# Reading and writing the 288 columns of every weight product from the last to the first

## The chip, the cores and the metric

The kernel runs on one core of one Trainium2 chip. The metric is the device time of one launch in microseconds (us). Before the change it is 2207.99 us, the median of three runs (2207.06 to 2208.8).

## The reference

The program computes one layer of a decoder trunk for two groups of tokens: a prompt of 256 tokens and a sample group of 8 x 4 = 32 tokens. With the width 2048 the layer is

```python
x = x + 0.5 * rmsnorm(swiglu(rmsnorm(x, g[0]), ffn1_w_in, ffn1_w_out), g[1])
m, sg, sh = hybrid_mixer(rmsnorm(x, g[2]), ...)     # gated linear attention (4 heads) and HGRN2 (8 heads)
x = x + rmsnorm(m, g[3])
x = x + 0.5 * rmsnorm(swiglu(rmsnorm(x, g[4]), ffn2_w_in, ffn2_w_out), g[5])
```

`swiglu(x, w_in, w_out)` is `(silu(gate) * up) @ w_out` with `gate, up = split(x @ w_in)` and an inner width of 5632. The mixer projects with `mix_w_in` (2048 to some 7200 columns), evaluates two recurrences over the tokens, normalises, gates, and projects back with `mix_w_out`. Outputs are the new activations of both groups and the final states of both recurrences. Everything is fp32, and the result has to be accurate to fp32 inputs.

## The kernel before

**Layout.** All 288 tokens (256 of the prompt, then 32 of the sample group) are handled together. Activations lie with the model dimension on the 128 partitions and the tokens along the row: `x[k]` is a 128 x 288 tile, k from 0 to 15. A weight product takes a 128 x 128 piece of a weight matrix as the stationary operand and a 128 x 288 activation tile as the moving operand, and accumulates 128 x 288 sums in a PSUM tile.

**Three products for one.** TensorE's reduced fp32 format (fp32r in the profile, `F32R` in the code) drops low bits. So each weight piece is split by ScalarE and VectorE into a high part and a low part (lines 100 and 101, tile `wh`), and so is each activation tile (`xh`, `xl` for the layer's input, `hh`, `hl` for the inner activations of the feed-forward part). `mm3` (lines 594 to 598) issues three products for each weight piece and activation tile: high x high (line 596), high weight x low activation (597) and low weight x high activation (598). All go into the same accumulator `dst`; the first of a chain starts the sum anew, the last closes it. The operands `parts[0]` and `parts[1]` are the whole rows of the high and the low tile, `dst` the first 288 columns of an accumulator of 512.

**Blocks.** `block` (from line 583) computes 512 output columns of a matrix: four accumulators of 128 output rows, and for each up to 16 steps over the inner dimension. When the last step of an accumulator is issued, `evac` reads it with VectorE or ScalarE. Blocks are named after what they compute, and these names stand in the profile: `gate`, `up` and `out` for the feed-forward parts, `qk`, `v`, `hfq`, `hi`, again `gate`, and `mo` for the mixer. `Fill.products` uses the same `mm3` for a few products that are issued early, at the border of two parts of the layer (names with `fill`). The scans of the recurrences, the transposes, the norms' sums and the small low-rank projection have product calls of their own, with lines of their own, among them line 437 (column sums for a norm), line 863 (sums at the end, in full fp32) and line 1385 (the sample group's state update, in fp32r).

**Order.** Weights come in units of 512 KB on SP's DMA queue, three raw units ahead (`Weights.fill`), and are split up to four units ahead of their use (`Weights.ahead`). The tile framework issues each engine's instructions by a planner from their dependencies and priorities; `tc.issue_after` puts some instructions behind others on the same engine by hand, and the `tick` callbacks spread the scans' work between the weight products.

Of the kernel before, what the change touches and what calls it, by code (L numbers as in the profile page):

```python
# [130 lines left out]
def trunk_kernel(ctx, tc, x_prompt, x_sample, state_gla, state_hgrn, norm_gains, f1_in, f1_out, f2_in, f2_out,  # L131
# [3 lines left out]
    V, S, G, PE = nc.vector, nc.scalar, nc.gpsimd, nc.tensor  # L135
# [33 lines left out]
    def mmtile(name):  # L169
        return mmp.tile([P, 512], F32, name=name, tag="mm")  # L170
# [416 lines left out]
    def block(name, nk, rhs, evac, width=512, tick=None, tail=1, hold=False, most=99, fill=None, late=0, byk=(), lag=0, skip=()):  # L587

        nf, per = width // P, 1024 // width
        nu = nk // per  # L590
        ps = [mmtile(f"{name}_{f}") for f in range(nf)]
        ws = [W.next() for _ in range(EARLY // per)] if fill else []

        def mm3(dst, w, f, k, parts, start, stop):
            a, c = k % per, slice(f * P, f * P + P)
            yield lambda: PE.matmul(dst, w[0][:, a, c], parts[0], start=start, stop=False)  # L596
            yield lambda: PE.matmul(dst, w[0][:, a, c], parts[1], start=False, stop=False)  # L597
            yield lambda: PE.matmul(dst, w[1][:, a, c], parts[0], start=False, stop=stop)  # L598

        def mm(w, f, k):  # L600
            if not fill or f or k >= EARLY:
                for ready in mm3(ps[f][:, 0:T], w, f, k, rhs(k), k == 0, k == nk - 1):
                    product[0] = ready().ins

        if fill:
            fill.products(lambda dst, k, parts, stop: mm3(dst, ws[k // per], 0, k, parts, k == 0, stop), ps[0][:, 0:T])
        for u in range(nu - tail):
            w = ws.pop(0) if ws else W.next()
            if u not in byk:
                for f in range(nf):  # L610
                    for k in range(u * per, (u + 1) * per):
                        mm(w, f, k)
                    if tick is not None and f % 2:
                        tick(u * per + f // 2)
            for k in range(u * per, (u + 1) * per) if u in byk else ():
                if fill and k < UPDATED:

                    fs = range(1 if k < EARLY else 0, nf)
                    threes = [list(mm3(ps[f][:, 0:T], w, f, k, rhs(k), k == 0, False)) for f in fs]
                    for three in threes:  # L620
                        three[0]()
                        product[0] = three[2]().ins
                    with tc.issue_after(product[0]):
                        for three in threes:
                            product[0] = three[1]().ins
                elif k < late:

                    threes = [list(mm3(ps[f][:, 0:T], w, f, k, rhs(k), k == 0, False)) for f in range(nf)]
                    for ready in [r for t in threes for r in t[:2]] + [t[2] for t in threes]:
                        product[0] = ready().ins  # L630
                else:
                    for f in range(nf):
                        mm(w, f, k)
                if tick is not None:
                    tick(k)
            if u not in skip and not (lag and u == nu - tail - 1):
                W.ahead(most)
            if fill and u == 5:
                fill.scaled()
        ws = [W.next() for _ in range(tail)]  # L640
        ks = range((nu - tail) * per, nk)
        ticked = 0
        for f in range(nf):
            for k in ks:
                mm(ws[k // per - (nu - tail)], f, k)
            ins = evac(f, fill.total(ps[f][:, 0:T]) if fill and f == 0 else ps[f][:, 0:T])
            while tick is not None and (ticked + 1) * nf <= (f + 1) * len(ks):
                tick(ks[ticked])
                ticked += 1
            if lag and f == lag:  # L650
                with tc.issue_after(ins):
                    W.ahead(most)
        if not hold:
            W.ahead()
# [1078 lines left out]
```

## Time and profile before

| | |
|---|---|
| median of three runs | 2207.99 us |
| span of the profiled execution, first to last instruction | 2206.5 us |
| mean granted TensorE clock | 1.000 |
| TensorE busy | 2198.2 us |
| VectorE busy | 1385.7 us |
| ScalarE busy | 1020.1 us |
| read from HBM | 363.75 MB |

The profile gives no other time of the profiled execution than its span; the span is 1.5 us below the median of the runs. In the rows that follow, PE is TensorE, PEld its weight loads, DVE is VectorE, ACT ScalarE and POOL GpSimd; L597 is line 597 of the kernel. A row of instructions by line gives the engine, the operation, the tile that is written and the tiles that are read, the count, and the shortest, median and longest duration. A row of the timeline gives the start, the duration, and what ran. Products overlap in the engine's pipeline and their ends are modelled, so the duration of one is longer than the distance from its start to the start of the next.

### The profile page before, as it was taken

How to read it: one execution, taken by the hardware profiler on the slowest of the kernel's cores; microseconds unless marked ns; L12 is line 12 of the kernel's file. 1: busy time of each engine (PE TensorE's matmuls, PEld its weight loads, DVE VectorE, ACT ScalarE, POOL GpSimd, SP SyncE). 2: the span in 40 equal slices, each digit the busy share in tenths (PEclk: the TensorE clock that was granted, in tenths of full speed). 3: DMA queues.
4: the chain of work that ended last, by engine and by line, in shares of the span. 5: the costliest groups of instructions: out<-in, count | busy, mean ns of one | idle time of the engine just before them, and what ended most of it. 6: DMA issues, size and time to landing. Idle time of an engine off the chain costs nothing.

```text
span 2206.5 us, 43225 instructions
## 1 busy us (share of the span) xinstructions
PE 2198.2 (100%) x17828; PEld 2182.2 (99%) x17828; DVE 1385.7 (63%) x2253; ACT 1020.1 (46%) x1537; POOL 180.0 (8%) x327
## 2 busy tenths in 40 slices
PE   9999999999999999999999999999999999999998
PEld 9999999999999999999999999999999999999998
DVE  7545546555555568888888755844555466556646
ACT  6443433343344345655676654543333333333344
POOL 2000000000000001233210000000000020122005
PEclk9999999999999999999999999999999999999999
DMA  7655555555555554667566564555555565666555
GB/s 223 174 166 171 169 168 170 171 165 171 172 166 180 179 166 142 194 207 216 173 189 176 176 190 135 169 167 171 171 166 170 172 176 172 180 179 179 172 164 161
DMA packets 227334, 384.87 MB, mean 174 GB/s; under 512 B 21362, under 2 KB 60864, under 8 KB 227136
## 3 DMA queue, kind: packets, MB, share of 16 engines
q1 hardware_dynamic: 213872, 365.02, 55.1%
q0 software_dynamic: 10992, 16.77, 2.8%
q8 instruction: 140, 2.29, 0.4%
q10 hardware_dynamic: 2272, 0.31, 0.1%
q14 instruction: 58, 0.48, 0.1%
HBM read 363.75 MB, written 11.80 MB: 170 GB/s over the span
## 4 chain that ended last, share of the span: by engine, by line
PE 98%; DVE 1%; ACT 1%; issue 0%; POOL 0%; DVEq 0%; ACTq 0%; POOLq 0%
PE gate L597 10%; PE gate L596 10%; PE gate L598 10%; PE up L597 8%; PE out L597 8%; PE up L596 8%; PE up L598 8%; PE out L596 8%; PE out L598 8%; PE hfq L596 2%; PE hfq L597 2%; PE mo L597 2%; PE hfq L598 2%; PE mo L596 1%; PE mo L598 1%; PE hi L597 1%
## 5 line engine op out<-in xcount | busy, mean ns | idle before, releaser
L101 DVE TENSOR_TENSOR wh<-raw,wh 128x1024 fp32r<-128x1024 f32 (+1 forms) x676 | 821.7, 1217 | 610.2 <-ACT wh L100 609.1
L100 ACT ACTIVATE wh<-raw 128x1024 fp32r<-128x1024 f32 (+1 forms) x676 | 711.0, 1053 | 943.1 <-PE gate L598 295.2
L597 PE MATMUL gate<-xl,wh 128*128 128x288 f32 x1660 | 490.1, 297 | 0.0
L598 PE MATMUL gate<-xh,wh 128*128 128x288 f32 x1660 | 483.6, 293 | 0.0
L596 PE MATMUL gate<-xh,wh 128*128 128x288 f32 x1660 | 483.0, 292 | 0.0
L597 PE MATMUL out<-hl,wh 128*128 128x288 f32 x1408 | 419.2, 298 | 0.0
L597 PE MATMUL up<-xl,wh 128*128 128x288 f32 x1408 | 419.2, 298 | 0.0
L598 PE MATMUL up<-xh,wh 128*128 128x288 f32 x1408 | 411.6, 292 | 0.0
L598 PE MATMUL out<-hh,wh 128*128 128x288 f32 x1408 | 411.5, 292 | 0.0
L596 PE MATMUL out<-hh,wh 128*128 128x288 f32 x1408 | 409.3, 291 | 0.0
L596 PE MATMUL up<-xh,wh 128*128 128x288 f32 x1408 | 409.3, 291 | 0.0
L596 PEld LDWEIGHTS gate<-xh,wh 128*128 128x128 f32 x1660 | 313.7, 189 | 0.8 <-DVE u L691 0.4
L598 PEld LDWEIGHTS gate<-xh,wh 128*128 128x128 f32 x1660 | 311.4, 188 | 0.2 <-DVE wh L101 0.2
L597 PEld LDWEIGHTS gate<-xl,wh 128*128 128x128 f32 x1660 | 310.2, 188 | 0.5
L596 PEld LDWEIGHTS out<-hh,wh 128*128 128x128 f32 x1408 | 266.8, 189 | 0.2 <-DVE y L782 0.2
L596 PEld LDWEIGHTS up<-xh,wh 128*128 128x128 f32 x1408 | 266.7, 189 | 0.0
L598 PEld LDWEIGHTS up<-xh,wh 128*128 128x128 f32 x1408 | 264.5, 188 | 0.0
L598 PEld LDWEIGHTS out<-hh,wh 128*128 128x128 f32 x1408 | 264.5, 188 | 0.0
L597 PEld LDWEIGHTS up<-xl,wh 128*128 128x128 f32 x1408 | 263.8, 187 | 0.0
L597 PEld LDWEIGHTS out<-hl,wh 128*128 128x128 f32 x1408 | 263.7, 187 | 0.0
L782 DVE TENSOR_TENSOR y<-out,y 128x288 f32<-128x288 f32 x287 | 120.7, 452 | 82.1 <-PE out L598 81.1
L739 POOL DMA_DIRECT2D xT<-b x64 | 37.1, 586 | 757.3 <-PE gate L598 566.7
(417 smaller groups left out, 2559.1 us busy)
## 6 DMA issues: line engine op xcount, KB each, us to landing
raw<-in_ffn_w_in_dram SPq DMA_DIRECT2D x350, 512.0 KB, 3.6
raw<-in_ffn_w_out_dram SPq DMA_DIRECT2D x176, 512.0 KB, 3.6
raw<-in_mix_w_in_dram SPq DMA_DIRECT2D x64, 512.0 KB, 4.3
raw<-in_mix_w_in_dram SPq DMA_DIRECT2D x96, 256.0 KB, 3.2
raw<-in_mix_w_out_dram SPq DMA_DIRECT2D x32, 512.0 KB, 3.7
out_dram<-s POOLq DMA_DIRECT2D x32, 256.0 KB, 2.9
s<-in_state_gla_dram SPq DMA_DIRECT2D x16, 256.0 KB, 5.9
s<-in_state_hgrn_dram SPq DMA_DIRECT2D x16, 256.0 KB, 5.6
```

What stands on the lines that cost most here:

```text
L100: i1 = self.nc.scalar.activation(h[:, a, c], raw[:, a, c], AF.Copy).ins
L101: i2 = self.nc.vector.tensor_tensor(l[:, a, c], raw[:, a, c], h[:, a, c].bitcast(F32), op=ALU.subtract).ins
L596: yield lambda: PE.matmul(dst, w[0][:, a, c], parts[0], start=start, stop=False)
L597: yield lambda: PE.matmul(dst, w[0][:, a, c], parts[1], start=False, stop=False)
L598: yield lambda: PE.matmul(dst, w[1][:, a, c], parts[0], start=False, stop=stop)
L739: queues[n % len(queues)].dma_start(dst[q * TS:(q + 1) * TS, 4 * g:4 * g + 4, :, cols].rearrange("p k t c -> p (k t) c"), b32[rows, q])
L782: V.tensor_tensor(y[k], ps, y[k], op=ALU.add)
```

## The change

In each of the three products of `mm3`, the moving operand and the accumulator are both given with their columns reversed. Column 287 is read first and its sum is written to column 287 first, then 286, down to 0. The same elements are multiplied and added in the same sums; the stationary operand is given as before. `mm3` serves all weight products of the layer, those of `Fill` included. Products with calls of their own are not touched.

```diff
         def mm3(dst, w, f, k, parts, start, stop):
             a, c = k % per, slice(f * P, f * P + P)
-            yield lambda: PE.matmul(dst, w[0][:, a, c], parts[0], start=start, stop=False)
-            yield lambda: PE.matmul(dst, w[0][:, a, c], parts[1], start=False, stop=False)
-            yield lambda: PE.matmul(dst, w[1][:, a, c], parts[0], start=False, stop=stop)
+            yield lambda: PE.matmul(dst[:, ::-1], w[0][:, a, c], parts[0][:, ::-1], start=start, stop=False)
+            yield lambda: PE.matmul(dst[:, ::-1], w[0][:, a, c], parts[1][:, ::-1], start=False, stop=False)
+            yield lambda: PE.matmul(dst[:, ::-1], w[1][:, a, c], parts[0][:, ::-1], start=False, stop=stop)
```

## The prediction

> **What bounds the kernel now.** I read the page's totals and the chain of waits first, then one steady stretch, then single products.
>
> ```profile
> span 2206.5 us, 43225 instructions
> PE 2198.2 (100%) x17828; PEld 2182.2 (99%) x17828; DVE 1385.7 (63%) x2253; ACT 1020.1 (46%) x1537; POOL 180.0 (8%) x327
> PEclk9999999999999999999999999999999999999999
> PE 98%; DVE 1%; ACT 1%; issue 0%; POOL 0%; DVEq 0%; ACTq 0%; POOLq 0%
> ```
>
> TensorE is idle for 2206.5 − 2198.2 = 8.3 us of the whole span, and the chain that ends last is 98% TensorE. Nothing else comes near: VectorE is busy for 63%, ScalarE for 46%. A busy share alone does not say how long a product really holds the engine, since products overlap in the pipeline. For that I take a window of the second feed-forward part, where nothing but weight products runs, and starts one after another:
>
> ```profile
> core 0: us, PE busy (x) PEld busy (x) DVE busy (x) ACT busy (x) POOL busy (x), PEclk, DMA share, GB/s
> 1430.00:2150.00 720.00, 720.00 (x5541) 720.00 (x5540) 397.62 (x551) 281.64 (x329) 45.85 (x80) 1.00 0.57 172
> ```
> ```profile
> 599.75 0.29 PE L596 MATMUL gate<-xh,wh 128*128 128x288 f32 x1
> 599.88 0.30 PE L597 MATMUL gate<-xl,wh 128*128 128x288 f32 x1
> 600.01 0.29 PE L598 MATMUL gate<-xh,wh 128*128 128x288 f32 x1
> ...
> 603.78 0.30 PE L597 MATMUL gate<-xl,wh 128*128 128x288 f32 x1
> ```
>
> 5541 products in 720 us are 0.1299 us each, and the starts, 31 products from 599.75 to 603.78, say 0.130. The row's 0.29 us is the time of one product from entry to the modelled end; its hold on the engine is 0.130. The granted clock of the window is 1.00, so a throttle plays no part.
>
> How many such products are there? The rows of line 597, the middle one of each three:
>
> ```profile
> L597 PE MATMUL gate<-xl,wh x1660: 288/298/402, 7.1 to 2118.3; 128*128 128x288 f32 x185
> L597 PE MATMUL up<-xl,wh x1408: 289/298/298, 36.0 to 2143.2; 128*128 128x288 f32 x176
> L597 PE MATMUL out<-hl,wh x1408: 292/298/298, 111.6 to 2193.4; 128*128 128x288 f32 x176
> L597 PE MATMUL hfq<-xl,wh x256: 290/297/378, 959.4 to 1147.5; 128*128 128x288 f32 x128
> L597 PE MATMUL mo<-xl,wh x256: 297/298/298, 1264.8 to 1364.2; 128*128 128x288 f32 x128
> L597 PE MATMUL v<-xl,wh x128: 289/297/298, 859.9 to 959.0; 128*128 128x288 f32 x128
> L597 PE MATMUL hi<-xl,wh x128: 290/296/404, 988.5 to 1087.5; 128*128 128x288 f32 x128
> L597 PE MATMUL qk<-xl,wh x124: 289/296/400, 842.0 to 921.8; 128*128 128x288 f32 x124
> L597 PE MATMUL qk<-fill2xl,wh x4: 296/297/379, 835.8 to 839.3; 128*128 128x288 f32 x4
> L597 PE MATMUL fill<-fill2yl,wh x4: 295/296/296, 839.7 to 840.9; 128*128 128x288 f32 x4
> L597 PE MATMUL gate<-fill4xl,wh x4: 292/298/380, 1366.0 to 1368.0; 128*128 128x288 f32 x4
> L597 PE MATMUL fill<-fill4yl,wh x4: 298/298/298, 1368.4 to 1369.6; 128*128 128x288 f32 x4
> ```
>
> They sum to 5384; lines 596 and 598 have as many each, so 16,152 products are touched. At 0.1299 us they fill 2098 us, 95% of the span. So the whole forecast is one number: by how much the 0.130 us of one product changes when its 288 columns are read and written in descending order. **Each nanosecond is worth 16,152 ns = 16.2 us, or 0.73%.** A change of 0.2%, about what a measurement of this kernel can tell from none, is a mere 0.27 ns.
>
> **The change, part by part.** *Instructions.* Nothing is added or removed: three products per weight tile, the same 128 x 128 weights, 288 columns, in the same order of calls. The same bytes are read and written, so no tile is touched that was not, and the waits that follow from overlap stay as they are: 0 us. The cover, should the issue order shift a little, is that TensorE's weight-product lines wait for next to nothing (8.3 us of idle time in all).
>
> *Evacuation.* VectorE and ScalarE read an accumulator only after its last product, and read it in ascending order as before; whether column 0 or column 287 was written last makes no difference to a wait on the instruction. 0 us.
>
> *The products.* No instruction of this kernel reads or writes backwards, so the trace has no row for it, and its price is bounded from both sides. Three rows bear on what sets 0.130 us. First a product with almost no columns, which shows what the weights alone cost:
>
> ```profile
> L437 PE MATMUL post<-onesD,acc x6: 249/250/271, 836.1 to 836.7; 128*128 128x1 f32 x6
> 836.11 0.83 PE L437 MATMUL post<-onesD,acc 128*128 128x1 f32 x6
> ```
>
> Six in 0.83 us with 0.25 for the last leave (0.83 − 0.25)/5 = 0.116 us from one to the next with a single column. That is the floor under every product with new weights, 14 ns below the 0.130. A gain is therefore at most 14 ns x 16,152 = 226 us. Second, a longer product of the same number format (fp32r), and third, products in full fp32:
>
> ```profile
> 1054.59 0.40 PE L1385 MATMUL sn<-bd,ks 96*128 96x512 f32 x1
> 1054.82 0.29 PE L596 MATMUL hfq<-xh,wh 128*128 128x288 f32 x1
> ```
> ```profile
> 2197.79 1.02 PE L863 MATMUL sum<-zT,diag 128*128 128x512 f32 x2
> 2198.65 1.02 PE L863 MATMUL sum<-xT,ident 128*128 128x512 f32 x2
> 2199.51 1.02 PE L863 MATMUL sum<-zT,diag 128*128 128x512 f32 x2
> ```
>
> 512 fp32r columns hold the engine for 0.23 us, 0.45 ns a column; 288 in 0.130 are 0.45 ns too. So the hold grows with the columns, and it is the stream of columns that sets it, not the weights: any slowing of the stream is seen in full, nothing hides it. The fp32 products take 0.86 us per two of 512, 0.43 each, or 0.84 ns a column. That is the slowest steady pace of columns in this trace and serves as the upper end: 288 x 0.84 = 242 ns, 112 ns more than now, 1809 us in all.
>
> Which value between −14 and +112 ns? The nearest row is the product itself, ascending, 0.130 us: same format, width, weights, tiles. [...] I take 0 ns. **Sum:** 2206.5 + 0 + 0 + 0 = 2206.5 us of span; the median of the runs shown is 2207.99, 1.5 us above this span, so the forecast on that scale is 2208 us.
>
> [...]
>
> **The rivals.**
>
> *Half pace (slower).* fp32r columns pass at 0.45 ns each where fp32 columns take 0.84, so the paths that feed and drain the array carry nearly twice as many columns per us in the weight products. If that rate rests on two neighbours being taken together, and a descending step defeats this on the reading or on the writing side, each column goes alone and the pace falls to that of the fp32 rows: 2208 + 1809 = about 4017 us. For it: 0.45 ns is above half of 0.84 (0.42), so fp32r already runs a little slower than twice the fp32 pace and some limit outside the array is in reach. Against it: the two neighbours are the same bytes in either order. It decides as soon as the hold passes 0.130 us, since no cover exists; a partial loss, one stalled access in several, would lie anywhere below 4017.
>
> *A small loss at each start.* From 288 columns in 0.130 us and 512 in 0.23, a column costs 0.10/224 = 0.446 ns and a product about 1.4 ns beside its columns. If setting up a descending walk, or the first access that starts at the end of a row, costs as much again, it is 1.4 x 16.2 = 23 us: 2231 us. Up to 16 ns, as a collision with the weight loads now and then, would be 2466 us. [...] Against: the interval hardly varies over 720 us of quite different neighbours.
>
> *A small gain.* The 0.45 ns lie 0.03 above half of the 0.84; if the surplus is a conflict of the ascending walk with the weight loads that a mirrored walk avoids, 0.03 x 288 = 9 ns go, 9 x 16.2 = 145 us: about 2063 us, and with half of it 2135. VectorE (398 of 720 us) and the DMA share (0.57) could follow. Against: nothing in the trace says that the surplus depends on direction.
>
> *Not done as said.* If both patterns were turned round again on the way to the instruction, the time is 2208 as well; it is in the first case's chance.
>
> **How the numbers follow.** No change 0.60 (the nearest row, and a mirrored walk over whole groups); half pace or a loss beyond 16 ns 0.20, the one asymmetry that the 0.45 against 0.84 makes plausible; a small loss 0.12; a gain 0.08. So faster 0.08, same 0.60, slower 0.32. The range takes in the no-change case, the small losses up to 16 ns (2466, rounded up to 2470), and gains down to half of the surplus (2135, rounded down to 2130), and leaves out the half pace and the fullest gain, some 0.2 to 0.22 together. The likeliest case's own range is 2204 to 2212 us.
>
> **What would show it.** Right: the starts in the 599.75 stretch again 0.130 us apart; 1430 to 2150 again holding about 5541 products; the same counts per line. Wrong towards half pace: starts near 0.24 us, TensorE as full as before, VectorE's share falling from 63% to about 35%, and the 512-column rows of L863 and L1385, which stay ascending, unchanged. A small loss would show as an interval of 0.131 to 0.146 in every stage alike; a shift in the order of instructions as idle time of TensorE in a few places, which would not be the columns' doing. The forecast is wrong if the interval moves by more than 0.3 ns, whatever the cause.

## The result and the profile after

The changed kernel takes **2238.72 us** (median of four runs, 2238.31 to 2239.62) against 2208.39 us of the kernel before (now four runs; the three shown ahead have the median 2207.99): slower by 1.38%, the ratio 1.0138 with a 95% interval of 1.0124 to 1.0152. Medians and ratios leave out a single run, a fourth of `shift64` with 4900.7 us, more than twice any other time here. The span of its profiled execution is 2237.8 us, 31.3 us more than before. From its page:

```profile
span 2237.8 us, 43224 instructions
PE 2228.7 (100%) x17828; PEld 2212.9 (99%) x17828; DVE 1385.6 (62%) x2253; ACT 1020.9 (46%) x1537; POOL 180.6 (8%) x327
PEclk9999999999999999999999999999999999999999
PE 97%; DVE 1%; DMA 1%; ACT 1%; issue 0%; SPq 0%; DVEq 0%; ACTq 0%
```

The counts of instructions on the engines are the same, VectorE and ScalarE are as busy as before (1385.6 and 1020.9 us), the clock row is the same. TensorE is idle for 9.1 us where it was 8.3. So the 31 us are more time in the same products. A three, below, is the three products of one `mm3`. The windows view, first three blocks one after another (gate, up and out, each window from the first start of one block to the first start of the next; a block is 64 threes, 192 products, and the counts have two or three neighbours that reach into the window), then the long window of the second feed-forward part:

```profile
core 0: us, PE busy (x), PEclk, DMA share, GB/s
605.42:630.80 25.38, 25.38 (x195) 1.00 0.58 168
630.80:656.19 25.39, 25.39 (x195) 1.00 0.52 164
656.19:681.57 25.38, 25.38 (x195) 1.00 0.58 166
1430.00:2150.00 720.00, 720.00 (x5447) 1.00 0.57 170
```

And three such blocks (up, out and gate) of the kernel before:

```profile
core 0: us, PE busy (x), PEclk, DMA share, GB/s
621.25:646.21 24.96, 24.96 (x194) 1.00 0.52 166
646.21:671.17 24.96, 24.96 (x194) 1.00 0.58 171
671.17:696.13 24.96, 24.96 (x194) 1.00 0.57 172
```

720 us now hold 5447 products where they held 5541: 132.2 ns from one start to the next, not 129.9. A block takes 25.38 or 25.39 us for 24.96, and a three, the 64th part, 396.7 ns for 390.0. Nearly all blocks take the same time to 0.01 us, before and after: the stream runs in a steady rhythm, and the changed kernel has another rhythm. The exceptions in these two kernels lie behind interruptions, and they matter further down. In the kernel before, the hi block at 988 us is one; 19 threes, nothing between them:

```profile
988.37:995.91 7.54, 7.54 (x59) 1.00 0.28 75
```

That is 397 ns a three, at the places in memory where most other blocks run at 390.0. The v block from 866 us begins the same way and falls into 390.0 after some 24 threes. So the ascending stream already knew the longer rhythm; in the changed kernel no block of 64 threes shows the shorter one.

Where the time went by stage follows from first and last starts on line 597 of the changed kernel:

```profile
L597 PE MATMUL gate<-xl,wh x1660: 292/297/402, 6.7 to 2147.7; 128*128 128x288 f32 x185
L597 PE MATMUL out<-hl,wh x1408: 293/297/297, 112.5 to 2224.1; 128*128 128x288 f32 x176
L597 PE MATMUL qk<-fill2xl,wh x4: 293/294/377, 848.7 to 852.1; 128*128 128x288 f32 x4
L597 PE MATMUL gate<-fill4xl,wh x4: 292/297/383, 1383.5 to 1385.5; 128*128 128x288 f32 x4
```

The first feed-forward part, from gate's first start to qk's, went from 835.8 − 7.1 = 828.7 to 842.0 us; the mixer, from there to the second gate's start, from 530.2 to 534.8; the second feed-forward part, to the last out, from 827.4 to 840.6. That is +13.3, +4.6 and +13.2 us, 31.1 together. The two feed-forward parts have 6336 products each, so 2.1 ns a product; the mixer's 3480 products, which the scans interrupt and which were in part at 397 ns a three before, lost 1.3 ns each.

### The profile page after: what moved, and what is told of

Read it like the earlier page. It is cut to its first block, busy times and chain, and to the rows that moved or that the text cites. A ratio compares the mean times of both kernels' runs of the same rounds, so it can differ in the third digit from the quotient of the medians.

```text
span 2237.8 us, 43224 instructions
## 1 busy us (share of the span) xinstructions
PE 2228.7 (100%) x17828; PEld 2212.9 (99%) x17828; DVE 1385.6 (62%) x2253; ACT 1020.9 (46%) x1537; POOL 180.6 (8%) x327
## 4 chain that ended last, share of the span: by engine, by line
PE 97%; DVE 1%; DMA 1%; ACT 1%; issue 0%; SPq 0%; DVEq 0%; ACTq 0%
PE gate L597 10%; PE gate L596 10%; PE gate L598 10%; PE up L597 8%; PE out L597 8%; PE out L596 8%; PE up L596 8%; PE up L598 8%; PE out L598 8%; PE hfq L596 2%; PE mo L597 2%; PE hfq L597 2%; PE mo L596 2%; PE hfq L598 1%; PE mo L598 1%; PE hi L597 1%
## 5 line engine op out<-in xcount | busy, mean ns | idle before, releaser
L596 PE MATMUL out<-hh,wh 128*128 128x288 f32 x1408 | 417.1, 296 | 0.0
L596 PE MATMUL up<-xh,wh 128*128 128x288 f32 x1408 | 416.9, 296 | 0.0
L598 PE MATMUL out<-hh,wh 128*128 128x288 f32 x1408 | 412.9, 293 | 0.0
L598 PE MATMUL up<-xh,wh 128*128 128x288 f32 x1408 | 412.8, 293 | 0.0
```

The lines of the kernel that those rows point to most:

```text
L596: yield lambda: PE.matmul(dst[:, ::-1], w[0][:, a, c], parts[0][:, ::-1], start=start, stop=False)
L598: yield lambda: PE.matmul(dst[:, ::-1], w[1][:, a, c], parts[0][:, ::-1], start=False, stop=stop)
```

## The experiments

Two things were open: on which side the cost sits, and whether the direction itself has a price. Four of the kernels run (`table1` to `table4`) are bench kernels, run once each for their trace; the others were timed against the kernel before. Three theories are named by letters: A, a fixed cost at the start of every descending product; B, a cost for each column read backwards; C, the column stream and the weight loads disturb each other, and the direction only shifts when.

**Reading alone, writing alone.** `read_only` keeps the reversed moving operand and writes ascending; `write_only` keeps the reversed accumulator and reads ascending (lines 597 and 598 in the same way):

```diff
-            yield lambda: PE.matmul(dst[:, ::-1], w[0][:, a, c], parts[0][:, ::-1], start=start, stop=False)
+            yield lambda: PE.matmul(dst, w[0][:, a, c], parts[0][:, ::-1], start=start, stop=False)          # read_only
+            yield lambda: PE.matmul(dst[:, ::-1], w[0][:, a, c], parts[0], start=start, stop=False)          # write_only
```

> Only the moving operand is read from the last column to the first; the accumulator is written ascending. Tokens are then mixed up between the columns, so the values are not the reference's, while the work is all there. If the cost sits on the reading side: 2239 us as with both reversed. If on the writing side: 2208 us. If the two sides share it: in between.

> Only the accumulator is written from the last column to the first; the moving operand is read ascending (values mixed up between the columns as in the run before). If the cost sits on the writing side: 2239 us. If on the reading side: 2208 us. A whole cost here and a whole cost in the run before as well would speak for a set-up of any descending pattern.

Measured: `read_only` 2238.05 us, ratio 1.0132 (1.0115 to 1.0149); `write_only` 2208.34 us, ratio 1.0001 (0.9992 to 1.0011). One block of each in the windows view:

```profile
604.95:630.34 25.39, 25.39 (x194) 1.00 0.51 166
```
```profile
622.01:646.97 24.96, 24.96 (x194) 1.00 0.51 168
```

The first is `read_only`, in the rhythm of the changed kernel, the second `write_only`, in that of the kernel before. All of the cost sits on the reading side. Writing the accumulator backwards cost nothing here, the ratio being 1.0001. Not every block of `write_only` is like the one shown. Its profiled execution took 2212.04 us, one of two of the ten near 2212, and it shows the longer rhythm for a while: at 390 ns a three up to 718 us, then a break in which two threes took 675 and 500 ns, then some 300 threes at 397 ns, up to 838 us. A gate and an up block of these:

```profile
736.86:762.24 25.38, 25.38 (x194) 1.00 0.52 167
762.24:787.63 25.39, 25.39 (x194) 1.00 0.50 166
```

No operand had moved, and the kernel before took 24.96 us for the same blocks. At one and the same place the ascending stream thus ran in either rhythm, 24.96 or 25.38 us a block, and here the longer one came in behind a break.

**One of the three lines.** `d598` reverses line 598 only, reading and writing:

```diff
-            yield lambda: PE.matmul(dst, w[1][:, a, c], parts[0], start=False, stop=stop)
+            yield lambda: PE.matmul(dst[:, ::-1], w[1][:, a, c], parts[0][:, ::-1], start=False, stop=stop)
```

> Only the third product of each three (low weight x high activation, line 598) is reversed, reading and writing. Theory A and B: a third of the cost, 0.6 ns on the average of a product, +10 us: 2218 us. Theory C: the distance from line 598 to the next 596 alone went down in the changed kernel (131 to 129 ns, where 596 to 597 rose from 126 to 133 and 597 to 598 from 133 to 135), so this run could lie anywhere from 8 us below the kernel before (the 598 to 596 gain alone) to 10 us above.

Measured: 2239.49 us, ratio 1.0139 (1.0124 to 1.0154). One product in three reversed costs as much as all three:

```profile
604.97:630.36 25.39, 25.39 (x194) 1.00 0.52 166
```

That is outside what each theory gave (2200 to 2218 us). A price per reversed product, be it at its start or per column, would have come to a third. Theories A and B fall here; C missed as well.

**The first bench table.** `table1` runs the threes in series, with nothing else going on.

> A bench kernel that leaves the whole layer out (its outputs are zeros): nothing but series of fp32r products with the weight tiles, activation tiles and the threes of the kernel, each series once ascending and once descending, with nothing else running. Read from each: the mean distance from one start to the next. Theory A (a fixed cost at the start of a descending product): descending minus ascending is about 1.9 ns in every series, whatever the width (256, 384, 512 columns), and for one and the same weight piece and activation tile too. Theory B (a stall per column, or per group of columns): the difference grows with the width, about 1.7 ns at 256, 2.5 at 384, 3.3 at 512. [...]

The rows of one line for series of 256, 384 and 512 columns, ascending (last letter a) and descending (d); first and last start are 31 threes apart:

```profile
L84 PE MATMUL nba<-bh,wh x32: 276/281/334, 344.0 to 355.1; 128*128 128x256 f32 x32
L84 PE MATMUL nbd<-bh,wh x32: 279/280/281, 355.4 to 366.5; 128*128 128x256 f32 x32
L84 PE MATMUL nca<-bh,wh x32: 336/336/339, 366.9 to 383.1; 128*128 128x384 f32 x32
L84 PE MATMUL ncd<-bh,wh x32: 338/341/344, 383.6 to 400.1; 128*128 128x384 f32 x32
L84 PE MATMUL nda<-bh,wh x32: 389/395/404, 400.7 to 422.2; 128*128 128x512 f32 x32
L84 PE MATMUL ndd<-bh,wh x32: 394/397/400, 422.9 to 444.6; 128*128 128x512 f32 x32
```

11.1 against 11.1, 16.2 against 16.5, 21.5 against 21.7 us: per product 0, +3 and +2 ns. The difference is neither constant nor does it grow with the width. With 288 columns, all eight mixes of directions came out between 397 and 403 ns a three (mean over the last two thirds of a series, from the starts of its products, as in all bench figures below), **the all-ascending one too**: 399 ns, not the kernel's 390. With 284 columns, ascending and descending took 390 and 390 ns from the start of the row, 383 and 397 from 16 bytes past it. By the sizes of the tiles in the order of their allocation, the rows of this bench started on a multiple of 128 bytes; those of the kernel start 64 bytes past one, the weights on a multiple in both. This made a further theory, of the address phase: the rhythm is set by where the bytes lie.

**Moving rows by 64 bytes, ascending.** `shift64` is the kernel before with one allocation moved, and every instruction in the same order on every engine:

```diff
+    cols = xpool.tile([P, 16], F32, name="cols")
     xh = [xpool.tile([P, T], F32R, name=f"xh{k}") for k in range(KT)]
...
-    cols = xpool.tile([P, 16], F32, name="cols")
```

> The kernel before, all ascending, with one change of addresses: the small tile cols is allocated ahead of the split activations instead of behind them, so that all rows of xh and xl start 64 bytes later, on a multiple of 128 instead of 64 past one. The weights and the rows of hh, hl and the fill tiles stay where they are. It touches 16,152 - 3 x 1408 = 11,928 products (the out products and a few fill products read the others). Theory of the address phase: these slow from 390 to about 397 ns a three as descending did, 11,928 x 2.2 ns = 26 us: about 2235 us, with out unchanged at 390. Theory of direction: 2208 us.

Measured: 2230.64 us, the median of three runs from 2229.7 to 2231.3, ratio 1.0099 (1.0079 to 1.0119), 4 us less than worked out. Two blocks that read the moved rows (gate, up), then the out block, whose rows stayed:

```profile
602.57:627.96 25.39, 25.39 (x194) 1.00 0.50 166
627.96:653.35 25.39, 25.39 (x195) 1.00 0.49 166
653.35:678.32 24.97, 24.97 (x193) 1.00 0.53 169
```

Nothing is reversed here, and the blocks with moved rows take the 25.39 us of the reversed kernel, while out keeps its 24.96. So the shorter rhythm can be lost with no descending read at all; an address does the same.

**Rows and weights together, weights alone, and descending rows moved.**

```diff
     gate = const.tile([P, 3], F32, name="gate")
+    pad64 = const.tile([P, 16], F32, name="pad64")                                   # all64: everything 64 bytes later
...
     hlp = ctx.enter_context(tc.tile_pool(name="hlp", bufs=HL_BUFS))
+    colsp = ctx.enter_context(tc.tile_pool(name="colsp", bufs=1))                     # wh64: weights 64 bytes earlier
...
-    cols = xpool.tile([P, 16], F32, name="cols")
+    cols = colsp.tile([P, 16], F32, name="cols")
```

> The kernel before, all ascending, with an unused tile of 64 bytes ahead of everything, so that the rows of xh, xl, hh and hl and the split weights all start 64 bytes later; the distance from rows to weights is kept (the 24 fill threes read rows that stay). If what counts is where the rows lie against the weights: 2208 us, where shift64, the rows alone, gave 2231. If what counts is where the rows lie by themselves: all products slow, some 2231 to 2243 us.

> The kernel before, all ascending, with the split weights and the raw weights alone moved by 64 bytes (the tile cols goes behind them); all rows stay. If the distance from rows to weights counts: all 16,152 products slow from 390 to between 397 and 402 ns a three, 16,152 x 2.2 to 4 ns = 36 to 65 us: 2244 to 2273 us. If the rows' own place counts: 2208 us.

> The changed kernel, all descending, with the rows of xh and xl moved by 64 bytes as in the run shift64. Theory of the address phase by a mirror (a descending row of 1152 bytes that starts on a multiple of 128 ends where an ascending one that starts 64 bytes past begins): back to 390 ns a three for gate, up and the mixer's products, about 2216 us. What the second table's series say (descending 397 at 0 and at 64 alike): no change, 2239 us. Theory of direction: 2239 us as well.

Measured: `all64` 2210.57 us, ratio 1.0011 (1.0002 to 1.0020); `wh64` 2239.05 us, ratio 1.0138 (1.0121 to 1.0155); `after_shift64`, the changed kernel with the allocation of `shift64`, 2249.92 us, ratio 1.0188 (1.0173 to 1.0204). A block of `all64`, a block of `wh64`, and gate, up and out of `after_shift64`:

```profile
620.70:645.66 24.96, 24.96 (x195) 1.00 0.50 170
```
```profile
605.71:631.09 25.38, 25.38 (x194) 1.00 0.52 166
```
```profile
607.72:633.32 25.60, 25.60 (x195) 1.00 0.51 164
633.32:658.92 25.60, 25.60 (x195) 1.00 0.49 166
658.92:684.30 25.38, 25.38 (x194) 1.00 0.53 166
```

`all64` moved the rows of `shift64` by the same 64 bytes and is fast, because the weights moved along: what counts is where the rows lie against the weights. `wh64`, with all rows in place, is as slow as the change under study, though 5 us below the least that was worked out. (Its weights moved 64 bytes down, not up; modulo 128 that is the same.) The distance was not kept everywhere. For a third of the last 44 weight units before each border of two parts, the split weights lie in a second pool (`begin_extra`), which is allocated from the other side and did not move. Just there blocks of `all64` leave 24.96 us, as this out block, which fits its ratio of 1.0011:

```profile
710.25:735.63 25.38, 25.38 (x194) 1.00 0.57 182
```

In `after_shift64` neither the mirror (2216 us) nor an unchanged 2239 us came out, but a third rhythm of 25.60 us, 400.0 ns a three; so descending rows are not indifferent to their place either.

| rows of xh, xl past a multiple of 128 bytes | weights past it | reading | most gate and up blocks, ns a three | time, us |
|---|---|---|---|---|
| 64 | 0 | ascending | 390.0 | 2208 |
| 0 | 64 | ascending (`all64`) | 390.0 | 2210.6 |
| 0 | 0 | ascending (`shift64`) | 396.7 | 2230.6 |
| 64 | 64 | ascending (`wh64`) | 396.7 | 2239.1 |
| 64 | 0 | descending (the change) | 396.7 | 2238.7 |
| 0 | 0 | descending (`after_shift64`) | 400.0 | 2249.9 |

**More bench tables.** `table2` scans the start of the rows in steps of 8 bytes, `table3` puts high and low rows and high and low weights at different places.

> The bench kernel again (the layer left out, outputs zeros), all series with 288 columns and the kernel's threes. Between the series the moving rows start 0, 8, 16, ... 120 bytes past a multiple of 128, each once ascending and once descending; the weights start on a multiple of 128 as in the kernel, in four series 64 bytes past it. Theory of the address phase: a three takes one of a few lengths, from some 384 to 400 ns, and which one depends on the start address; ascending at 64 bytes past (the kernel's own place) gives about 390 ns, ascending at 0 about 397 (as the first table's ascending series, whose rows start there), descending at 64 about 397, and there are other addresses at which descending falls to 390 or below. Theory of direction: descending gives about 397 at every address and ascending about 390.

Mean length of a three over the last two thirds of each series:

| bytes past a multiple of 128 | 0 | 16 | 32 | 48 | 64 | 80 | 96 | 112 | odd multiples of 8 |
|---|---|---|---|---|---|---|---|---|---|
| ascending, ns | 400 | 399 | 399 | 397 | 397 | 410 | 401 | 394 | 398 to 407 |
| descending, ns | 397 | 397 | 397 | 398 | 397 | 397 | 397 | 400 | 403 to 407 |

(Ascending at 0 is from a later series; the first ran while its operands were still arriving and never had more than 12 products in a row.) With the weights at 64 past, rows at 0 ascending gave 390 and rows at 64 gave 400, as `all64` and `wh64` later did in kind. At several places descending is the shorter of the two, by 13 ns at 80 bytes: a fixed price of the direction is ruled out. The theory missed in two places: no descending address fell to 390, and ascending at 64 gave 397, in a later series too, where the kernel has 390.

> The bench kernel (the layer left out, outputs zeros), ascending threes of 288 columns. 64 series set the high rows and the low rows 0, 16, ... 112 bytes past a multiple of 128, each by itself, against weights on a multiple of 128; 16 more move the high and the low weights against rows at 64 past. If the distance of rows to weights picks one of a few lengths: values from about 384 to 410 ns a three, with some below the 390 of the kernel, and none of them outside; the four ways of having rows and weights 64 bytes apart near 390. If it is the kernel's 390 that can't be beaten: none below 388.

The first of the 80 ascending series ran while its operands were arriving; the other 79 lay between 390 and 410 ns. None is clearly below the kernel's 390, so this table points to no place that would beat it. The kernel's own place modulo 128, rows at 64 and weights at 0, came twice and gave 399 ns both times, where `table2` had 397 both times at the same addresses. Bytes modulo 128 are thus not the whole rule, and the two programs differ in something besides these addresses (they also ran on different chips).

**The kernel's own addresses.** `table4` puts rows and weights at the very addresses of the kernel, and varies the number of weight columns.

> The bench kernel (the layer left out, outputs zeros), now with the high rows, the low rows and the weights at the very addresses that they have in the kernel before. First 16 series with 288 columns and full weights: rows moved by 0, 16, ... 112 bytes from the kernel's place, ascending and descending. If the addresses are the whole cause and the other engines have no part: 390 ns a three ascending at 0, 397 descending at 0, 395 to 400 ascending at 64, 397 to 403 descending at 64. If the work of other engines is needed for the 390: some other length at 0. Then 16 series in which the stationary operand has 32, 64, 96 or 128 columns, rows at 0 and 64, ascending and descending. [...] If the stream itself pays for direction or place: the same 130 and 132 ns at 32 columns as at 128.

Rows of one line for six series: with 128 weight columns ascending (daz) and descending (ddz) at the kernel's place, the same with the rows 64 bytes later (dah, ddh), then with 32 weight columns, ascending at the kernel's place (aaz) and 64 bytes later (aah):

```profile
L75 PE MATMUL colsdaz<-big,wh x32: 292/298/298, 411.1 to 423.2; 128*128 128x288 f32 x32
...
L75 PE MATMUL colsddz<-big,wh x32: 295/297/297, 423.6 to 435.9; 128*128 128x288 f32 x32
...
L75 PE MATMUL colsdah<-big,wh x32: 294/295/297, 436.3 to 448.6; 128*128 128x288 f32 x32
...
L75 PE MATMUL colsddh<-big,wh x32: 293/294/297, 449.0 to 461.4; 128*128 128x288 f32 x32
...
L75 PE MATMUL colsaaz<-big,wh x32: 293/296/298, 258.7 to 271.0; 128*32 128x288 f32 x32
...
L75 PE MATMUL colsaah<-big,wh x32: 288/290/294, 284.1 to 296.2; 128*32 128x288 f32 x32
```

31 threes in 12.1, 12.3, 12.3 and 12.4 us are 390, 397, 397 and 400 ns: the four timed kernels (before, changed, `shift64`, `after_shift64`) in one table, with next to no other work on the core. Addresses and direction were enough to bring these lengths about; the layer's traffic of DMA, VectorE and ScalarE was not needed. They do not fix the length alone, as the hi block and `write_only` showed. (An earlier ascending series at the kernel's place, at the head of the table, ran while its operands were arriving, in a run whose granted clock is 0.942 on the mean, and is not used. The first 16 series also had the other three of these four combinations, and agree to 0.2 ns.) At the remaining places of those 16 series, ascending took 393 to 403 ns and descending 394 to 400.

The second 16 series, by the number of weight columns (which also sets how many rows of the accumulator are written), in ns a three:

| weight columns | kernel's place, ascending | descending | 64 bytes later, ascending | descending |
|---|---|---|---|---|
| 32 | 397 | 397 | 390 | 397 |
| 64 | 397 | 397 | 397 | 397 |
| 96 | 397 | 403 | 398 | 397 |
| 128 | 390 | 397 | 397 | 400 |

With 32 columns the loads are shorter, 107 or 108 ns a row of PEld against 0.19 us with 128 columns, and yet ascending threes of 397 and 390 ns are no shorter than the 397 and 390 with 128: place still matters, and the spread does not grow steadily with the columns. But the size of the load does change which place is the good one, the one 64 bytes later with 32 columns (390 against 397 ns) and the kernel's with 128 (390 against 397), and with 32 or 64 columns the direction cost nothing at the kernel's place (397 both ways).

## Why the prediction was right or wrong

*What bounds the kernel, and the lever.* Right. The whole difference is the distance between the starts of the weight products; a nanosecond on each is worth 16.2 us, and 31.3 us of span are 1.94 ns. Nothing hid it.

*Instructions, evacuation.* Right at 0: every engine issues the same instructions in the same order, and `write_only` prices the accumulator's new order at nothing.

*The products: "I take 0 ns".* This is the term that was wrong, by 1.94 ns on the average and 2.2 ns in the steady blocks (396.7 against 390.0 ns a three). The likeliest case, 2208 us, did not come, and by the prediction's own sign, an interval that moves by more than 0.3 ns, the forecast of no change was wrong. That 2239 us lies in the range of 2130 to 2470 says little for the mechanism: the range was wide and took in losses up to 16 ns. The 0 was an estimate of mine, from the nearest row and from a mirrored walk over whole groups; no run shows such groups, and what the runs showed in place of the 0 is 2.2 ns a product. Nor was 130 ns a price of the walk alone. It is a third of the length of a rhythm that depended on where the rows lay against the weights (24.96 us a block in `all64`, 25.38 in `wh64`), and that was not even the only one at its place (390.0 and 397 ns in the kernel before). Read backwards, the stream stayed out of the shorter one: 396.7 ns, with the sum of the products 31 us longer. What I had read as a good sign, that the interval hardly varies over 720 us, was the mark of this rhythm. I treated the neighbouring row, the ascending product, as if its value held for every address, though the hi and v blocks of the same trace, which begin at 397 ns a three, could have told me that this value was not fixed.

*The rivals.* Half pace did not happen: 132 ns lie far from 242. The small loss, given 0.12, came near in size, 23 us worked out and 30 measured, but by coincidence, since its reason fell: a set-up cost of each descending product would have made `d598` a third as dear, and it was as dear as the whole (ratio 1.0139 against 1.0138). The remark beside it, a collision with the weight loads, is nearest to what the runs show, with one reservation: that the weights' place counts is shown (`wh64` 2239.05 us, `all64` 2210.57), and that the size of their load changes which place is good (`table4`, 32 against 128 columns); that their load and the column stream collide in the memory is not, since a load of 32 columns brought no distance below 390 ns a three. Moving the weights alone by 64 bytes lengthened a three from 390.0 to 396.7 ns, so the time of the stream did depend, by 1.7%, on where the weights lay. The small gain rested on the surplus over half of the fp32 pace going away in a mirrored walk; it grew, from 129.9 to 132.2 ns a product over the 720 us. The floor of 116 ns was read from products of a single column in full fp32; fp32r products of 128 columns in `table1` start 112 ns apart, so it is not a floor for these. Nothing hung on it.

*What stays open.* Why the lengths are 390.0, 396.7 and 400.0 ns, why a move by 64 bytes turns one into another, and why the same places modulo 128 gave 390 at the kernel's addresses and 397 to 399 at others. It is also open what picks the rhythm where a place showed two: a stretch behind an interruption began near 397 and fell into 390.0 later (v), another stayed at 396.7 for some 300 threes (`write_only`); what caused the break there is open too. No place was found at which a descending stream of 288 columns reaches 390; the shortest in the benches is 394.

## What to carry to other kernels

When products run back to back, measure them by the distance from start to start, to a nanosecond, over a whole block; the duration of a single one said little (medians of 297 and 298 ns on line 597 for two rhythms). This kernel was tuned to its addresses, knowingly or not: an edit that moves a tile or turns an access round cost 1.0% (`shift64`) to 1.4% (`wh64`, `read_only` 1.3%) with no instruction added, and an edit that seems to have a price should be run once with its tiles 64 bytes further on before the price is put down to it. Reversing the order in which an accumulator is written cost nothing here (1.0001); reversing the reading had no fixed price (at 80 bytes in `table2` it was 13 ns a three shorter), but with 288 columns it came to the shortest rhythm at no place that was tried (394 ns at best, against 390).

## What was not expected of the hardware

- The column stream of fp32r products took about 0.45 ns a column (130.0 ns for 288 in the kernel before, 231 ns for 512 in `table1`, ascending), more than half of the 0.84 of fp32 (line 863, 0.43 us for 512), and the lengths came in steps: nearly all uninterrupted blocks of the nine timed kernels took 24.96, 25.39 or 25.60 us, to 0.01 us, which is 390.0, 396.7 or 400.0 ns a three, the second and third two and three steps of 3.3 ns above the first.
- One product of three that reads backwards set the rhythm of all three: 25.39 us a block in `d598`, as with all three reversed.
- 64 bytes between rows and weights, in a kernel of 2.2 ms, were worth 31 us (`wh64`).
- At the same addresses a stream ran in two rhythms: 390.0 ns a three in the kernel before and 396.7 in `write_only`, for the same gate and up blocks.
